# Spreading routing weights per token with two float32r products instead of one float32 product

## The chip, the cores and the metric

The kernel runs on one core of one Trainium2 chip. The metric is the device time of one execution in microseconds (us). An execution uses TensorE (PE, with its weight loads shown as PEld), VectorE (DVE), ScalarE (ACT), GpSimd (POOL) and SyncE (SP), which issues the transfers.

## The reference

Two transformer blocks in sequence on x of 256 tokens by 1024 features: a first block of two attention layers, then a second block with one attention layer and a PEER layer, a mixture of 16384 experts that are one neuron each. The change lies in the PEER layer, of which this is what is computed, with PEER_HEADS 8, PEER_KEYS 128 and PEER_TOPK 16:

```python
def chunk(xc):
    qh = (xc @ w_query).reshape(PEER_CHUNK, PEER_HEADS, PEER_QDIM)
    s1 = jnp.einsum('thd,hnd->thn', qh[..., :PEER_HALF], sub_keys[:, 0]).astype(jnp.float32)
    s2 = jnp.einsum('thd,hnd->thn', qh[..., PEER_HALF:], sub_keys[:, 1]).astype(jnp.float32)
    v1, i1 = lax.top_k(s1, PEER_TOPK)
    v2, i2 = lax.top_k(s2, PEER_TOPK)
    cand = (v1[..., :, None] + v2[..., None, :]).reshape(PEER_CHUNK, PEER_HEADS, PEER_TOPK * PEER_TOPK)
    vs, ci = lax.top_k(cand, PEER_TOPK)
    e1 = jnp.take_along_axis(i1, ci // PEER_TOPK, axis=-1)
    e2 = jnp.take_along_axis(i2, ci % PEER_TOPK, axis=-1)
    idx = e1 * PEER_KEYS + e2
    g = jax.nn.softmax(vs, axis=-1)
    u_sel = u_experts[idx]
    v_sel = v_experts[idx]
    z = jnp.einsum('td,thkd->thk', xc, u_sel)
    a = (jax.nn.gelu(z.astype(jnp.float32)) * g).astype(xc.dtype)
    return jnp.einsum('thk,thkd->td', a, v_sel)
```

Every token thus has 128 chosen experts (8 heads of 16), each with two indices e1 and e2 below 128 and a weight g.

## The kernel before

The kernel gathers no expert rows. It computes the PEER layer densely, for all 16384 experts, and multiplies by a matrix of weights that is zero where an expert was not chosen. One **u block** (`u_tile`, from line 1314) takes one value of e1: it loads the 128 rows of u with that e1 (512 KB), splits them into a high and a low float32r part (ACT makes `hi`, line 186, DVE makes `lo`, line 211, in two halves of 128x512), runs 24 products of 256 columns on PE (lines 239 to 241) and applies gelu on ACT (line 1322). The result, 128 values of e2 by 256 tokens, stays in `GA` for e1 below KA = 72. For the other 56 values it goes into a ring of tiles `ge`, and a transfer writes it to memory (`spill`, line 1366, transfer on line 1369).

Once the routing is done, the weights are **spread** (lines 1483 to 1504). For four tokens at a time, 64 groups in all, DVE compares a row of numbers 0 to 127 (`iof`) with the token's indices: `o2` (line 1489) holds ones where e2 fits and `o1` (line 1490, bfloat16) where e1 fits, with the 128 chosen slots on the partitions. ACT multiplies `o1` by the weights, one activation of 128x128 per token, into `og` (line 1492). PE multiplies `o2` by `og`, one float32 product of 128 columns per token (line 1493), which the chip runs as two instructions: the profile shows 512 of them for 256 tokens. The four tokens' results lie in one PSUM tile `ps`. DVE multiplies its first 72 values of e1 into `GA` (line 1496), and ACT copies the other 56 to `GB` (line 1497).

While this stage runs, PE also computes the u blocks that are left: after each group or two the loop on line 1498 asks for one more `spill`. The stretch in which groups and u blocks alternate is called **the stage** below. After it come the products with v, one value of e1 after the other.

A scheduler sets the order on each engine from the priorities in program order and the dependences between tiles, and each engine then runs its own list in order. A ring of tiles has a number of buffers (`bufs`); the writer of a buffer waits until its last reader is done. `o1`, `o2` and `og` have two buffers of four tokens each, `hi` and `lo` four each.

Of the kernel before, what the change touches and what calls it, by code (L numbers as in the profile page):

```python
# [9 lines left out]
F32 = mybir.dt.float32  # L10
F32R = mybir.dt.float32r
# [3 lines left out]
AF = mybir.ActivationFunctionType  # L15
OP = mybir.AluOpType
# [133 lines left out]
class Net:  # L150
# [1184 lines left out]
    def peer(self, r4, h):  # L1335
        nc, v, a = self.nc, self.nc.vector, self.a
# [13 lines left out]
        eT = [tp.tile([128, 256], F32, name=f"eT{i}") for i in range(2)]  # L1350
        gT = tp.tile([128, 256], F32, name="gT")
# [5 lines left out]
        def uu(n):  # L1357
            while n and self.nu < KA + KS:
                if self.nu < KA:
                    self.u_tile(self.nu, h, GA[:, self.nu, :])  # L1360
                else:
                    spill()
                self.nu += 1
                n -= 1

        def spill():
            ge = self.wp.tile([128, 256], F32, name="ge", tag="ge", bufs=3)
            self.u_tile(self.nu, h, ge)
            nc.sync.dma_start(zd[self.nu - KA], ge)
        with ExitStack() as er:  # L1370
            self.wp = self.pool("wr", stack=er)
            wp = self.wp
# [108 lines left out]
        self.wp = self.pool("wa", stack=eg)  # L1481
        wp = self.wp
        iob = iof[:, None, :].to_broadcast([128, 4, 128])
        for t0 in range(0, S, 4):
            ps = self.ps()
            o2 = wp.tile([128, 4, 128], F32, name="o2", tag="o2", bufs=2)
            o1 = wp.tile([128, 4, 128], BF, name="o1", tag="o1", bufs=2)
            og = wp.tile([128, 4, 128], F32, name="og", tag="og", bufs=2)
            v.tensor_tensor(o2, iob, eT[1][:, t0:t0 + 4, None].to_broadcast([128, 4, 128]), op=OP.is_equal)
            v.tensor_tensor(o1, iob, eT[0][:, t0:t0 + 4, None].to_broadcast([128, 4, 128]), op=OP.is_equal)  # L1490
            for j in range(4):
                nc.scalar.activation(og[:, j], o1[:, j], AF.Copy, scale=gT[:, t0 + j:t0 + j + 1])  # L1492
                nc.tensor.matmul(ps[:, j * 128:j * 128 + 128], o2[:, j], og[:, j], start=(j == 0), stop=(j == 3),  # L1493
                                 skip_group_check=True)
            pv = ps.rearrange("p (t e) -> p e t", t=4)
            v.tensor_tensor(GA[:, :, t0:t0 + 4], pv[:, 0:KA], GA[:, :, t0:t0 + 4], op=OP.mult)
            nc.scalar.copy(GB[:, :, t0:t0 + 4], pv[:, KA:])
            n = N_E1 - 2
            if self.nu < n and (self.nu - KA - KS) * S <= t0 * (n - KA - KS):
                spill()  # L1500
                self.nu += 1
        while self.nu < N_E1:
            spill()
            self.nu += 1
# [10 lines left out]
        for e1 in range(N_E1):  # L1515
            for e in range(max(KA, e1 + 1), min(N_E1, e1 + NGE)):
                if e not in spilled:

                    ge = spilled[e] = wp.tile([128, 256], F32, name="ge", tag="ge", bufs=NGE)
                    nc.sync.dma_start(ge, zd[e - KA])  # L1520
            if e1 == 8:
# [11 lines left out]
                for c in range(2):  # L1533
                    ps = self.ps()
# [4 lines left out]
            else:  # L1539
                A = spilled.pop(e1)  # L1540
                i = v.tensor_tensor(A, A, GB[:, e1 - KA, :], op=OP.mult)
# [131 lines left out]
```

## Time and profile before

| | |
|---|---|
| median of 3 runs | 1414.01 us (1412.24 to 1414.22) |
| the profiled execution's own time | 1413.74 us |
| its span, first to last instruction | 1412.0 us |
| PE busy over the span | 1366.8 us, 97% |
| DVE busy | 1023.2 us, 72% |
| ACT busy | 821.9 us, 58% |
| POOL busy | 21.9 us, 2% |
| mean granted clock of PE | 0.992 |
| transfers `zd<-ge`, issue to landing, median | 1.7 us |

A row of a timeline has the start in us from the start of the span, the duration in us (of all of them, where several are merged), the engine, the line, the operation, the tiles as output<-inputs without their numbers, the shape, and xN for N merged instructions; in brackets stands how long the engine had been idle and what ended that. A row on a source line has minimum, median and maximum duration in ns. The work on PE is pipelined: durations of neighbouring products overlap, so the price of a product in a stream is the distance between starts.

### The profile page before, as it was taken

What the parts mean: (1) busy time and instruction counts of PE and PEld (TensorE: products, weight loads), DVE (VectorE), ACT (ScalarE), POOL (GpSimd) and SP (SyncE); (2) the same over time, 40 slices, a digit from 0 to 9 for tenths busy, and PEclk for the clock granted to TensorE, in tenths of its full rate; (3) what the DMA queues carried; (4) which work ended last, traced back from release to release, by engine and by line L of the source; (5) the groups of instructions that cost most, each with busy time, mean ns of one, the idle gap of its engine ahead of it and who ended that gap; (6) DMA issues with size and microseconds to landing.
All of it is one profiled execution on the core that took longest, in us unless ns stands there. A gap on an engine that the chain in (4) does not pass through costs nothing.

```text
span 1412.0 us, 24444 instructions
## 1 busy us (share of the span) xinstructions
PE 1366.8 (97%) x8522; PEld 1120.8 (79%) x8522; DVE 1023.2 (72%) x2636; ACT 821.9 (58%) x1887; POOL 21.9 (2%) x27
## 2 busy tenths in 40 slices
PE   6999999999989998999999999999999999999997
PEld 2566666477767755999999999999998888888885
DVE  3585756388665656799999968888866666677777
ACT  2353656357646654555555568888865555555554
POOL 0000000000001100000000000000000000000001
PEclk9999999999999999999999999999999999999999
DMA  8577564553486766455555555554456665677773
GB/s 309 199 272 273 197 203 138 199 186 101 138 313 199 216 225 223 135 182 179 179 179 179 181 188 193 165 164 162 165 194 227 194 194 194 194 227 239 245 242 114
DMA packets 94875, 279.15 MB, mean 198 GB/s; under 512 B 11112, under 2 KB 30320, under 8 KB 94624
## 3 DMA queue, kind: packets, MB, share of 16 engines
q1 hardware_dynamic: 94752, 277.59, 59.6%
q8 instruction: 67, 1.10, 0.3%
q14 instruction: 56, 0.46, 0.1%
HBM read 267.80 MB, written 13.94 MB: 200 GB/s over the span
## 4 chain that ended last, share of the span: by engine, by line
PE 90%; DVE 4%; DMA 4%; ACT 1%; issue 1%; SPq 0%; ACTq 0%; DVEq 0%
PE ps L240 18%; PE ps L239 18%; PE ps L241 18%; PE acc L240 5%; PE acc L239 5%; PE acc L241 5%; PE psa L393 5%; PE ps L1493 4%; PE ps L706 2%; DMA raw<-in_w1o 1%; PE ps L725 1%; PE ps L701 1%; PE psa L365 1%; DMA adaw<-in_adaw 1%; DVE lo L211 1%; PE ps L631 1%
## 5 line engine op out<-in xcount | busy, mean ns | idle before, releaser
L186 ACT CAST hi<-raw 128x512 fp32r<-128x512 f32 (+1 forms) x700 | 429.4, 618 | 349.9 <-PE ps L240 147.1
L211 DVE TENSOR_TENSOR lo<-raw,hi 128x512 fp32r<-128x512 f32 (+1 forms) x700 | 479.8, 688 | 179.7 <-ACT hi L186 162.8
L239 PE MATMUL ps<-hh,hi 128*128 128x256 f32 x1160 | 333.0, 287 | 1.3 <-DVE hh L187 1.3
L240 PE MATMUL ps<-hl,hi 128*128 128x256 f32 x1160 | 328.3, 283 | 1.1 <-DVE hl L211 1.1
L241 PE MATMUL ps<-hh,lo 128*128 128x256 f32 x1160 | 328.4, 283 | 0.0
L239 PEld LDWEIGHTS ps<-hh,hi 128*128 128x128 f32 x1160 | 222.6, 192 | 1.5 <-issue 1.5
L240 PEld LDWEIGHTS ps<-hl,hi 128*128 128x128 f32 x1160 | 222.4, 192 | 1.3 <-DVE hl L211 1.3
L241 PEld LDWEIGHTS ps<-hh,lo 128*128 128x128 f32 x1160 | 222.2, 192 | 0.0
L239 PE MATMUL ps<-hi,Ah 128*128 128x512 f32 x508 | 198.1, 390 | 0.0
L240 PE MATMUL ps<-lo,Ah 128*128 128x512 f32 x508 | 197.7, 389 | 0.0
L241 PE MATMUL ps<-hi,Al 128*128 128x512 f32 x508 | 197.6, 389 | 0.0
L239 PEld LDWEIGHTS ps<-hi,Ah 128*128 128x128 f32 x508 | 95.4, 188 | 20.1 <-issue 0.2
L241 PEld LDWEIGHTS ps<-hi,Al 128*128 128x128 f32 x508 | 95.4, 188 | 19.9
L240 PEld LDWEIGHTS ps<-lo,Ah 128*128 128x128 f32 x508 | 95.4, 188 | 19.9 <-DVE lo L211 0.2
L1492 ACT ACTIVATE og<-o,gT 128x128 f32<-128x128 bf16 x256 | 87.2, 394 | 4.1 <-DVE o L1490 0.3
L393 PE MATMUL psa<-adaw,cond 128*32 128x512 f32 x320 | 81.3, 610 | 3.1 <-DMA adaw<-in_adaw 3.1
L240 PE MATMUL acc<-lo,hh 128*128 128x512 f32 (+1 forms) x176 | 70.7, 402 | 2.4 <-DVE lo L211 2.4
L239 PE MATMUL acc<-hi,hh 128*128 128x512 f32 (+1 forms) x176 | 69.6, 401 | 2.6 <-DVE hh L187 1.4
L241 PE MATMUL acc<-hi,hl 128*128 128x512 f32 (+1 forms) x176 | 69.9, 398 | 0.0
L1493 PE MATMUL ps<-og,o 128*128 128x128 f32 x512 | 65.2, 275 | 0.1
L1493 PEld LDWEIGHTS ps<-og,o 128*128 128x128 f32 x512 | 61.4, 192 | 0.3 <-ACT og L1492 0.3
L733 ACT ACTIVATE P<-P,nm 128x128 f32<-128x128 f32 (+1 forms) x96 | 42.6, 446 | 13.5 <-DVE nm L730 13.4
(397 smaller groups left out, 1929.8 us busy)
## 6 DMA issues: line engine op xcount, KB each, us to landing
raw<-in_u SPq DMA_DIRECT2D x128, 512.0 KB, 3.6
raw<-in_v SPq DMA_DIRECT2D x128, 512.0 KB, 4.3
adaw<-in_adaw SPq DMA_DIRECT2D x86, 512.0 KB, 4.9
raw<-in_w SPq DMA_DIRECT2D x48, 512.0 KB, 4.3
raw<-in_wq SPq DMA_DIRECT2D x16, 512.0 KB, 3.4
zd<-ge SPq DMA_DIRECT2D x56, 128.0 KB, 1.7
ge<-zd SPq DMA_DIRECT2D x56, 128.0 KB, 3.6
raw<-in_adaw SPq DMA_DIRECT2D x10, 512.0 KB, 7.0
```

The lines of the kernel that those rows point to most:

```text
L186: return self.nc.scalar.copy(out, in_)
L211: return self.nc.vector.tensor_tensor(lo, src, hi.bitcast(F32), op=OP.subtract)
L239: mm(out, a[0][asl], b[0][bsl], start=first, stop=False, **kw)
L240: mm(out, a[0][asl], b[1][bsl], start=False, stop=False, **kw)
L241: mm(out, a[1][asl], b[0][bsl], start=False, stop=last, **kw)
L365: nc.tensor.matmul(ps[32 * q:32 * q + 32], self.cond[:, k, :], raw[:, j * 512:(j + 1) * 512], start=(k == 0), stop=(k == NK - 1), tile_pos ...
L393: nc.tensor.matmul(ps[32 * q:32 * q + 32], self.cond[:, ci + k, :], raw[:, j * 512:(j + 1) * 512], start=(k == 0), stop=(k == NK - 1), til ...
L631: nc.tensor.transpose(pr[:P, i * 128:i * 128 + 128], s.rearrange("p a d -> p (a d)") if P == 128 else s, self.identr)
L706: nc.tensor.matmul(o[64 * a:64 * a + 64], v[br][kb][:, 2 * pair + a, :], pts[a], start=first, stop=False, tile_position=(0, 64 * a), skip_ ...
L733: nc.scalar.activation(Pb, Pb, AF.Exp, scale=-1.0, bias=nm[:, r, br:br + 1], accum_out=sums[:, r, br:br + 1])
L1492: nc.scalar.activation(og[:, j], o1[:, j], AF.Copy, scale=gT[:, t0 + j:t0 + j + 1])
L1493: nc.tensor.matmul(ps[:, j * 128:j * 128 + 128], o2[:, j], og[:, j], start=(j == 0), stop=(j == 3), skip_group_check=True)
```

## The change

The float32 product of a token becomes two float32r products onto the same sums: `o2` times the high part of the weighted `o1`, then `o2` times the low part. `o2` is written as float32r.

- The weights `gT` are split once into `gh` and a low part, which replaces `gT` in place.
- ACT makes the high part, as before one activation per token, now from `gh` into a tile `ogh` of one token with a ring of four buffers.
- POOL makes the low part `ogl`, four tokens in one instruction of 128x512, in a ring of two buffers.
- `o1` is written ahead of `o2`.
- The ring of `ge` has two buffers instead of three.

```diff
-            ge = self.wp.tile([128, 256], F32, name="ge", tag="ge", bufs=3)
+            ge = self.wp.tile([128, 256], F32, name="ge", tag="ge", bufs=2)
...
+        gh = wp.tile([128, 256], F32R, name="gh")
+        self.split_to(gh, gT.bitcast(F32R), gT)
+        gh, gl = gh.bitcast(F32), gT
         for t0 in range(0, S, 4):
             ps = self.ps()
-            o2 = wp.tile([128, 4, 128], F32, name="o2", tag="o2", bufs=2)
+            o2 = wp.tile([128, 4, 128], F32R, name="o2", tag="o2", bufs=2)
             o1 = wp.tile([128, 4, 128], BF, name="o1", tag="o1", bufs=2)
-            og = wp.tile([128, 4, 128], F32, name="og", tag="og", bufs=2)
+            og = wp.tile([128, 4, 128], F32R, name="ogl", tag="ogl", bufs=2)
+            v.tensor_tensor(o1, iob, eT[0][:, t0:t0 + 4, None].to_broadcast([128, 4, 128]), op=OP.is_equal)
             v.tensor_tensor(o2, iob, eT[1][:, t0:t0 + 4, None].to_broadcast([128, 4, 128]), op=OP.is_equal)
-            v.tensor_tensor(o1, iob, eT[0][:, t0:t0 + 4, None].to_broadcast([128, 4, 128]), op=OP.is_equal)
+            nc.gpsimd.tensor_tensor(og, o1, gl[:, t0:t0 + 4, None].to_broadcast([128, 4, 128]), op=OP.mult)
             for j in range(4):
-                nc.scalar.activation(og[:, j], o1[:, j], AF.Copy, scale=gT[:, t0 + j:t0 + j + 1])
-                nc.tensor.matmul(ps[:, j * 128:j * 128 + 128], o2[:, j], og[:, j], start=(j == 0), stop=(j == 3),
-                                 skip_group_check=True)
+                oh = wp.tile([128, 128], F32R, name="ogh", tag="ogh", bufs=4)
+                nc.scalar.activation(oh, o1[:, j], AF.Copy, scale=gh[:, t0 + j:t0 + j + 1])
+                for i, g in enumerate((oh, og[:, j])):
+                    nc.tensor.matmul(ps[:, j * 128:j * 128 + 128], o2[:, j], g, start=(j == 0 and i == 0),
+                                     stop=(j == 3 and i == 1), skip_group_check=True)
```

On PE, the list has a place where two groups follow one another without a u block between them; there are 14 such pairs. These are the rows of one pair before (`ps_9943` and `ps_9959` are the two groups, `ps_9906` and `ps_9976` the u blocks around them):

```order
L241 MATMUL ps_9906<-hh_5763,lo_9926 128x256
L1493 MATMUL ps_9943<-og_9946,o2_9944 128x128 [waits DVE_49,Activation_49]
L1493 MATMUL ps_9943<-og_9946,o2_9944 128x128 [waits Activation_49] x3
L1493 MATMUL ps_9959<-og_9962,o2_9960 128x128 [waits DVE_49,Activation_49]
L1493 MATMUL ps_9959<-og_9962,o2_9960 128x128 [waits Activation_49] x3
L239 MATMUL ps_9976<-hh_5763,hi_9979 128x256 [waits PE_49]
```

The same place now, the first group `ps_9991` and the head of the second, `ps_10016`:

```order
L1499 MATMUL ps_9991<-ogh_9998,o2_9992 128x128 [waits DVE_49,Activation_49]
L1499 MATMUL ps_9991<-ogl_9994,o2_9992 128x128 [waits Pool_49]
L1499 MATMUL ps_9991<-ogh_10002,o2_9992 128x128 [waits Activation_49]
L1499 MATMUL ps_9991<-ogl_9994,o2_9992 128x128
L1499 MATMUL ps_9991<-ogh_10006,o2_9992 128x128 [waits Activation_49]
L1499 MATMUL ps_9991<-ogl_9994,o2_9992 128x128
L1499 MATMUL ps_9991<-ogh_10010,o2_9992 128x128 [waits Activation_49]
L1499 MATMUL ps_9991<-ogl_9994,o2_9992 128x128
L1499 MATMUL ps_10016<-ogh_10023,o2_10017 128x128 [waits DVE_49,Activation_49]
L1499 MATMUL ps_10016<-ogl_10019,o2_10017 128x128 [waits Pool_49]
```

Groups and u blocks keep their places on PE: 50 places with a group or a pair, and 49 u blocks of 24 products between them. Each token has a high and a low product, and the first low product of a group waits for POOL.

On ACT, these are the rows before that make the weights of the pair (`og_9946` and `og_9962`); `ge_9851` is the gelu of the second u block ahead of the pair, and `ps_9889` is the group that stands between the two u blocks:

```order
L1492 ACTIVATE og_9946<-o1_9945,gT_5858 128x128 [waits DVE_49,PE_49]
L1492 ACTIVATE og_9946<-o1_9945,gT_5858 128x128 x2
L1497 COPY GB_9704<-ps_9835 128x56x4 [waits DVE_49]
L1492 ACTIVATE og_9946<-o1_9945,gT_5858 128x128
L186 CAST hi_9979<-raw_9977 128x512 [waits DMAHW4_49,PE_49]
L186 CAST hi_9995<-raw_9977 128x512 [waits PE_49]
L1322 ACTIVATE ge_9851<-ps_9852 128x256 [waits PE_49]
L1492 ACTIVATE og_9962<-o1_9961,gT_5858 128x128 [waits PE_49]
L1492 ACTIVATE og_9962<-o1_9961,gT_5858 128x128 x2
L1497 COPY GB_9704<-ps_9889 128x56x4 [waits DVE_49]
L1492 ACTIVATE og_9962<-o1_9961,gT_5858 128x128
```

And now (`ogh_9998` to `ogh_10010` are the first group of the pair, `ogh_10023` to `ogh_10035` the second; `ge_9953` is the gelu of the u block directly ahead of the pair):

```order
L1497 ACTIVATE ogh_9998<-o1_9993,gh_9711 128x128 [waits PE_49]
L1497 ACTIVATE ogh_10002<-o1_9993,gh_9711 128x128 [waits PE_49]
L1497 ACTIVATE ogh_10006<-o1_9993,gh_9711 128x128 [waits PE_49]
L1497 ACTIVATE ogh_10010<-o1_9993,gh_9711 128x128 [waits PE_49]
L1503 COPY GB_9704<-ps_9928 128x56x4 [waits DVE_49]
L186 CAST hi_10108<-raw_10106 128x512 [waits DMAHW7_49,PE_49]
L186 CAST hi_10124<-raw_10106 128x512 [waits PE_49]
L1322 ACTIVATE ge_9953<-ps_9954 128x256 [waits DMAHW4_49,PE_49]
L1497 ACTIVATE ogh_10023<-o1_10018,gh_9711 128x128 [waits PE_49]
L1497 ACTIVATE ogh_10027<-o1_10018,gh_9711 128x128 [waits PE_49]
L1497 ACTIVATE ogh_10031<-o1_10018,gh_9711 128x128 [waits PE_49]
L1497 ACTIVATE ogh_10035<-o1_10018,gh_9711 128x128 [waits PE_49]
```

The weights of a pair's second group stood behind the gelu of the second u block ahead of the pair. Now they stand behind the gelu of the u block directly ahead of it, and each activation has a wait for PE.

On DVE, this is the stretch of the same pair now (before, line 1490 for the groups to come stood behind the second line-1496 multiplication, not between the two, and did not wait for POOL):

```order
L1502 TENSOR_TENSOR GA_5855<-ps_9991,GA_5855 128x72x4 [waits PE_49]
L1493 TENSOR_TENSOR o2_10080<-iof_5859,eT1_5857 128x512 [waits DVE_49]
L1492 TENSOR_TENSOR o1_10144<-iof_5859,eT0_5856 128x512 [waits Activation_49,Pool_49]
L1502 TENSOR_TENSOR GA_5855<-ps_10016,GA_5855 128x72x4 [waits PE_49]
L1493 TENSOR_TENSOR o2_10143<-iof_5859,eT1_5857 128x512 [waits DVE_49]
L1492 TENSOR_TENSOR o1_10207<-iof_5859,eT0_5856 128x512 [waits Activation_49,Pool_49]
L211 TENSOR_TENSOR lo_10172<-raw_10169,hi_10171 128x512 [waits DMAHW2_49,PE_49,Activation_49]
```

The number of DVE instructions in the stage is the same but for the one split of `gT`. On POOL, which had nothing in the stage, there are now 64 multiplications of 128x512 in a row. SP's list of transfers is the same.

## Rows read from the trace of the kernel before

**Rows 1.** Busy time by stretch, sum of four stretches from 845 to 1045.

```profile
sum 200.00, PE 199.92 PEld 199.75 DVE 164.99 ACT 163.91 POOL 0.00; mean PE 49.98 PEld 49.94 DVE 41.25 ACT 40.98 POOL 0.00
```

**Rows 2.** Chain of waits from 815 to 1050: start, us, what, xN merged.

```profile
861.39 1.78 PE ps L1493 x16
...
926.12 0.89 PE ps L1493 x8
929.89 0.89 PE ps L1493 x8
...
1034.08 1.78 PE ps L1493 x16
```

**Rows 3.** Timeline of PE and PEld in early stages: float32r products of few columns.

```profile
328.30 0.56 PE L725 MATMUL ps<-kT,qT 128*128 128x128 f32 x4
137.11 1.87 PEld L878 LDWEIGHTS ps<-kT,qT 128*128 128x128 f32 x16
98.18 0.87 PE L631 MATMUL ps<-identr,qhl 128*128 128x128 f32 x8
```

**Rows 4.** Timeline of PE and ACT around the pair that starts at 933.49.

```profile
933.49 1.95 PE L1493 MATMUL ps<-og,o 128*128 128x128 f32 x16
933.63 0.62 ACT L186 CAST hi<-raw 128x512 fp32r<-128x512 f32 x1 [0.78 <-PE ps L240]
934.15 0.38 ACT L1322 ACTIVATE ge<-ps 128x256 f32<-128x256 f32 x1
934.58 0.99 ACT L1492 ACTIVATE og<-o,gT 128x128 f32<-128x128 bf16 x3
```

**Rows 5.** Timeline of ACT, a gelu with weights right behind it.

```profile
855.89 0.38 ACT L1322 ACTIVATE ge<-ps 128x256 f32<-128x256 f32 x1
856.17 0.98 ACT L1492 ACTIVATE og<-o,gT 128x128 f32<-128x128 bf16 x3
```

**Rows 6.** The first pair: chain of waits, then timelines of PE and ACT.

```profile
847.43 3.40 DMA zd<-ge
848.73 1.95 PE L1493 MATMUL ps<-og,o 128*128 128x128 f32 x16
850.92 0.35 ACT L1497 COPY GB<-ps 128x224 f32<-128x224 f32 x1 [2.94 <-DMA zd<-ge]
```

**Rows 7.** Timeline of DVE in the pair of rows 4.

```profile
934.89 0.45 DVE L1496 TENSOR_TENSOR GA<-ps,GA 128x288 f32<-128x288 f32 x1
935.26 0.68 DVE L1489 TENSOR_TENSOR o<-iof,eT 128x512 f32<-128x512 f32 x1
935.86 0.45 DVE L1496 TENSOR_TENSOR GA<-ps,GA 128x288 f32<-128x288 f32 x1
```

**Rows 8.** POOL's multiplications and additions: lines 1568 and 1107 by source line.

```profile
L1568 POOL TENSOR_TENSOR raw<-xr,gf x2: 1300/1302/1305, 1397.6 to 1399.5; 128x512 f32<-128x512 f32 x2
L1107 POOL TENSOR_TENSOR bb<-bb,cst x16: 636/642/1096, 453.4 to 492.9; 128x256 f32<-128x256 f32 x16
```

**Rows 9.** POOL and DVE at once, 487 to 494: timelines, and line 211 there.

```profile
487.47 1.09 POOL L1107 TENSOR_TENSOR bb<-bb,cst 128x256 f32<-128x256 f32 x1
488.52 1.09 POOL L1107 TENSOR_TENSOR bb<-bb,cst 128x256 f32<-128x256 f32 x1
L211 DVE TENSOR_TENSOR lo<-raw,hi x4: 890/1014/1124, 487.2 to 490.3; 128x512 fp32r<-128x512 f32 x4
490.61 2.89 POOL L1107 TENSOR_TENSOR bb<-bb,cst 128x256 f32<-128x256 f32 x4
491.65 0.70 DVE L1306 TENSOR_TENSOR ps<-ps,ona 128x512 f32<-128x512 f32 x1 [0.45 <-ACT osq L1305]
```

**Rows 10.** POOL and DVE at once near the end, timelines, and line 274 everywhere.

```profile
1401.67 1.27 POOL L1568 TENSOR_TENSOR gf<-xr,gf 128x512 f32<-128x512 f32 x1 [0.84 <-DVE rx L272]
1401.81 1.15 DVE L274 SCALAR_TENSOR_TENSOR rx<-rx 128x1 f32<-128x1 f32 x1
L274 DVE SCALAR_TENSOR_TENSOR rx<-rx x10: 211/219/1150, 13.7 to 1405.9; 128x1 f32<-128x1 f32 x10
```

## The prediction

> **What bounds the kernel now.** I read the busy time by stretch first, to see which engine has no slack while the routing weights are spread. From 845 to 1045 PE is busy 199.92 of 200 us, DVE 164.99, ACT 163.91 and POOL not at all [rows 1]. The chain of waits says the same and gives the beat: a group of four tokens takes 0.89 us on PE, single groups start 3.77 us apart, so a u block takes 2.88, and a pair takes 1.78 [rows 2]. Of these long pieces there are 13 from 861.39 to 1034.08, and the timeline has one more at 848.73 [rows 6]. The stage is thus 64 groups of 0.89 and 49 u blocks of 2.88, 57.0 + 141.1 = 198.1 us. A microsecond lost or won by PE here is one of the kernel's time; DVE has some 35 us to spare, ACT as much. Anything that makes PE wait, or that adds more than 35 us to DVE's list, shows in the end.
>
> **PE's own work.** A float32 product is two instructions, and a group's eight take 0.89 us, 0.111 each [rows 2]. The change also issues eight per group, float32r of 128 columns. The trace has just this form: four in a row last 0.56, the last of them 0.22 as its single ones do, so (0.56 - 0.22)/3 = 0.113 from start to start. With 16 columns it is no less: sixteen weight loads in 1.87, the last 0.19, so 1.68/15 = 0.112 [rows 3]. Columns do not set it; the load of the weights does, and it is repeated where two products in a row share them, as line 878's do (one `qT` for two `kT`); the low product will load `o2` again. I take +0.001 for each of 512, **+0.6 us**, with 0 and +1 as ends.
>
> **ACT's list and the ring `ogh`.** The 256 activations keep their shape, so they cost what they cost; the split of `gT` adds one instruction on ACT and one on DVE ahead of the stage, where both wait for PE: nothing. But `ogh` holds four tokens, not eight. The weights of the next group can only be made when PE has used those of the last, and in the new list the second group of a pair stands behind the gelu of the u block directly ahead. Singles have time: 2.88 us of u block. For a pair, count from PE's start T = 933.49 [rows 4]. ACT's cast starts at T + 0.14 and the gelu at T + 0.66; weights follow a gelu by 0.28 where nothing else holds them [rows 5], so at T + 0.94. The first lasts 0.40, the next follow every 0.295 ((0.99 - 0.40)/2). PE could start the second group at T + 0.89 and now starts at about T + 1.37, and then goes by 0.295 a token instead of 0.22, three times 0.07. That is 0.48 + 0.22 = 0.70 us a pair. In the first pair ACT stands at the copy of `GB`, which is done only once the transfer has landed, until 850.92 [rows 6]; behind it now come two casts and a gelu (0.25 + 0.52 + 0.52 + 0.28) before the second group's weights at 852.5, ready at 852.9, where PE wanted them at 848.73 + 0.89 = 849.62: 3.3 us. The ring alone thus costs 13 x 0.70 + 3.3 = **12.4 us**; if a pair's weights started as soon as PE lets go of the buffers, it would be some 0.25 a pair, 6.5 in all, the low end.
>
> **POOL beside DVE.** This decides. POOL's 64 instructions take 1.30 us each alone (128x512), 83 us where it has nothing else to do [rows 8], and each low part is asked for a u block or more before PE needs it. Its own time is hidden. What it does to DVE is not. While POOL's additions and the `lo` subtractions ran together, the two took turns: POOL's starts are 1.05 apart, its instructions grew from 0.642 to 1.09 and DVE's from 0.69 to 1.01 [rows 8, 9]. A DVE instruction of one column even lasted 1.15 instead of 0.219 because POOL held it [rows 10]. An instruction with one input in PSUM went past POOL untouched, 0.70 [rows 9]. So `o1`, `o2` and `lo`, all with two inputs in SBUF, take turns with POOL, and the multiplication into `GA` does not. One turn of POOL with 256 columns and one `lo` take 1.05, and `lo` alone takes 0.60 (the step of such instructions in [rows 7]), so POOL adds 0.45; 256 columns more add 1.302 - 0.642 = 0.66 [rows 8]. I take **1.10 us** of DVE's time per POOL instruction.
>
> The Trainium skill, on the page "SBUF — State Buffer" (Who interferes with whom), says that the pair of ports which VectorE's second input and GpSimd share is an exclusive lock for the whole instruction. By that each POOL instruction would cost DVE its whole 1.30 us, and the sum below would end 64 x 0.20 = 12.8 us later, at 1452; the turns above show that some 0.2 overlaps, and I go by them.
>
> DVE's list in the stage: 64 x (0.37 + 0.60 + 0.60) for `GA`, `o2`, `o1` [rows 7] and 98 `lo` of 0.60 are 159.3 us. POOL adds 64 x 1.10 = 70.4, together 229.7. Some `GA` run in POOL's shadow, because the same end of a group releases both: the second of each pair and those before DVE falls behind, some 20 x 0.37 = 7.4. That leaves 222.3. In the first pair DVE stands some 3.1 us with ACT, which can't be used: 225.4. DVE starts the stage ahead by what a single group leaves, about 1.5 us (its weights are ready at T + 2.2 of 3.77): 223.9. Against 198.1 that is **+25.8 us**.
>
> This replaces the ring's 12.4 rather than adding to it. Single groups alone would just fit: four instructions of 0.60 and one POOL turn with `GA` in its shadow are 3.50 to 3.60 of 3.77. But a pair asks DVE for 6 x 0.60 + 2 x 1.10 + 0.37 = 6.2 in 4.66 + 0.70 = 5.36 us. DVE is then late, its `GA` no longer falls into POOL's shadow, singles take 2.4 + 1.1 + 0.37 = 3.87, and the delay grows instead of shrinking. It reaches PE through ACT: the copy of `GB` waits for `GA`, and behind that copy stand casts, gelu and weights. So PE's waits at the pairs should grow from 0.7 to some 2 us.
>
> **The rest.** `o1` ahead of `o2`: both are made two groups or more ahead, nothing. `ge` with two buffers: a write lands after 1.7 us, and the next use of its buffer comes two u blocks later, over 5.7 us: nothing, unless SP is late by 4 us. SP's list is unchanged.
>
> Sum: 1413.74 (the profiled execution, 0.3 under the median shown) + 25.8 = **1439.5 us**.
>
> **The rivals.**
> 1. *Only the ring costs.* If POOL's turns fit into the 35 us that DVE has spare and into `GA`'s shadow (all 64: 23.7 us, so 229.7 - 23.7 = 206.0), the pairs bound: 12.4 + 0.6, 1426.7. For it: singles just fit. Against: the pairs do not.
> 2. *POOL is heavier* than its rows: its input is bfloat16 and its weight a broadcast, which no row shows. At 1.30 per turn and no `GA` hidden it is +20, 1460; at twice the length POOL itself becomes the beat and it is far more.
> 3. *Faster: float32r loads weights quicker.* Eight transposes in float32r, also 128 columns, take 0.87, the last 0.25: 0.089 each [rows 3]. At that rate the 512 products take 45.6 us instead of 57.0; were the ring and POOL hidden, 1413.7 - 11.4 = 1402.3. It decides if an ordinary product behaves like these; the row of line 725 says it does not. The Trainium skill has a rule of this kind on the page "TensorE: Matmul & The Clock Gate" (Back-to-back issue gap): pairs of load and product of 128 columns sustain about 81 ns. By it the products would take 41.5 us and the kernel 1398, an estimate; the trace's 113 ns speaks against it.
> 4. *No change*: PE's work is the same, and POOL and the ring are hidden by buffers that I judge too small: 1414.
>
> **How the numbers follow.** About 0.2% is what a measurement here can tell from no change. Forecast 0.56, ring only 0.22, POOL heavier 0.11, no change 0.05, faster 0.06. So faster 0.06, same 0.05, slower 0.89. The range runs from the ring's low end, 1413.7 + 6.5 = 1420, to just under rival 2's first price, 1458; it leaves out the faster case, no change and most of the heavy POOL, some 0.18.
>
> **What would show it.** Right: 512 float32r products at 0.112 apart; POOL busy over 83 us and each instruction well over 1.30; `o1`, `o2`, `lo` longer than 0.69; PE idle at the pairs, released by ACT's weights, growing over the first pairs; DVE nearly without idle time. Wrong: DVE's durations unchanged (then rival 1), PE waiting for POOL in single groups (rival 2), or products closer than 0.1 (rival 3).

## The result: slower by 0.9%, and the profile after

The changed kernel took 1428.29 us, median of 5 runs (1422.86 to 1430.27); the kernel before took 1414.01, now also of 5 (1412.24 to 1415.94). The ratio is 1.0094, 95% interval 1.0071 to 1.0117. That is slower, inside the range of 1420 to 1458, and 11.2 us under the forecast of 1439.5. Rival 1, in which only the ring costs, had 1426.7. The profiled execution took 1428.72 us, its span 1427.0.

The page of the changed kernel begins with busy time, share of the span and instructions of each engine:

```profile
PE 1375.7 (96%) x8522; PEld 1129.3 (79%) x8522; DVE 1053.7 (74%) x2637; ACT 821.3 (58%) x1888; POOL 100.5 (7%) x91
```

DVE gained 30.5 us against the table ahead, and POOL 78.6. The busy time by stretch, summed over 845 to 1045, answers to [rows 1]:

```profile
sum 200.00, PE 193.89 PEld 192.04 DVE 183.41 ACT 153.68 POOL 72.43; mean PE 48.47 PEld 48.01 DVE 45.85 ACT 38.42 POOL 18.11
```

PE, which had no idle time here, now waits 6.1 us, and DVE is not full. The list of waits from 845 to 1065 (total us, times, longest) names what PE waits for:

```profile
POOL ogl L1494 <- PE ps L1499: 112.7, 40, 17.8
...
PE ps L1499 <- ACT ogh L1497: 6.4, 14, 2.3
ACT GB L1503 <- DVE GA L1502: 4.9, 14, 0.8
```

Fourteen waits, one for each pair, all for ACT's weights, none for DVE or POOL. In a pair the timeline of PE and ACT reads:

```profile
913.74 0.22 PE L1499 MATMUL ps<-ogh,o 128*128 128x128 f32 x1
...
914.35 0.38 ACT L1322 ACTIVATE ge<-ps 128x256 f32<-128x256 f32 x1
914.47 0.28 PE L1499 MATMUL ps<-ogl,o 128*128 128x128 f32 x1
914.62 1.56 ACT L1497 ACTIVATE ogh<-o,gh 128x128 fp32r<-128x128 bf16 x5
...
915.07 0.33 PE L1499 MATMUL ps<-ogh,o 128*128 128x128 f32 x1 [0.32 <-ACT ogh L1497]
...
919.14 0.22 PE L1499 MATMUL ps<-ogh,o 128*128 128x128 f32 x1
```

From PE's start T = 913.74 the weights follow the gelu at T + 0.88, and PE starts the second group at T + 1.33. The forecast had T + 0.94 and T + 1.37. The next group starts at T + 5.40, where a pair and a u block took 1.78 + 2.88 = 4.66 [rows 2]: 0.74 us a pair, where the forecast had 0.70. It is the same at each of the 13 later pairs and does not grow.

In the first pair the timelines of ACT and PE answer to [rows 6], and the stretches behind them show PE's granted clock (the column after POOL's):

```profile
852.31 0.34 ACT L1503 COPY GB<-ps 128x224 f32<-128x224 f32 x1 [2.88 <-DMA zd<-ge]
854.32 0.33 PE L1499 MATMUL ps<-ogh,o 128*128 128x128 f32 x1 [2.27 <-ACT ogh L1497]
```

```profile
854.00:856.00 2.00, 1.68 (x13) 1.69 (x14) 2.00 (x5) 2.00 (x8) 0.00 (x0) 1.00 0.54 125
856.00:858.00 2.00, 2.00 (x13) 2.00 (x12) 2.00 (x4) 1.30 (x4) 1.04 (x1) 0.56 0.80 286
858.00:860.00 2.00, 2.00 (x13) 2.00 (x13) 1.00 (x2) 0.18 (x2) 0.00 (x0) 0.59 0.05 17
860.00:862.00 2.00, 2.00 (x20) 2.00 (x19) 1.39 (x3) 2.00 (x7) 1.04 (x1) 1.00 0.14 49
```

PE waited 2.27 us for the weights, and about 4 us of the next u block then went at a clock of 0.56 to 0.59, near the lower of its two levels, 1.2 of 2.4 GHz: 13 products in each 2 us, where 0.12 us from one to the next would make 16 or 17. That costs some 1.4 us more. The stage lasts 211.7 us (847.3 to 1059.0) instead of 198.2 (845.0 to 1043.2), 13.5 more: 13 x 0.74, 2.3 and 1.4 are 13.3 of them. It also began 2.3 us later, behind code that the change does not touch.

What POOL does to DVE shows in the same pair, timelines of DVE and POOL:

```profile
914.48 0.69 DVE L211 TENSOR_TENSOR lo<-raw,hi 128x512 fp32r<-128x512 f32 x1 [0.42 <-ACT hi L186]
914.83 1.24 POOL L1494 TENSOR_TENSOR ogl<-o,gT 128x512 fp32r<-128x512 bf16 x1 [2.53 <-PE ps L1499]
915.09 0.45 DVE L1502 TENSOR_TENSOR GA<-ps,GA 128x288 f32<-128x288 f32 x1
915.45 1.16 DVE L1493 TENSOR_TENSOR o<-iof,eT 128x512 fp32r<-128x512 f32 x1
```

POOL starts when PE is done with a group, because only then is its buffer free. DVE's next instruction is `GA`, released by the same event, with one input in PSUM, and it keeps its 0.45 us. Only `o2` behind it is held, until POOL ends at 916.07. Over the stage (845 to 1060, instructions by line: busy us, mean ns) nothing else on DVE grew:

```profile
L1493 DVE TENSOR_TENSOR o<-iof,eT 128x512 fp32r<-128x512 f32 x62 | 75.4, 1217 | 0.0
L211 DVE TENSOR_TENSOR lo<-raw,hi 128x512 fp32r<-128x512 f32 x101 | 68.1, 685 | 20.4 <-ACT hi L186 20.4
```

`o2` went from 681 ns in the kernel before to 1217: 0.53 us per group, where the forecast had 1.10 per POOL instruction.

### The profile page after: what moved, and what is told of

Its sections match the earlier page's. It is cut to its first block, busy times and chain, and to the rows that moved or that the text cites. A ratio compares the mean times of both kernels' runs of the same rounds, so it can differ in the third digit from the quotient of the medians.

```text
span 1427.0 us, 24570 instructions
## 1 busy us (share of the span) xinstructions
PE 1375.7 (96%) x8522; PEld 1129.3 (79%) x8522; DVE 1053.7 (74%) x2637; ACT 821.3 (58%) x1888; POOL 100.5 (7%) x91
## 4 chain that ended last, share of the span: by engine, by line
PE 90%; DMA 4%; DVE 4%; ACT 2%; issue 1%; SPq 0%; ACTq 0%; DVEq 0%
PE ps L239 18%; PE ps L240 18%; PE ps L241 18%; PE acc L240 5%; PE acc L239 5%; PE acc L241 5%; PE psa L393 5%; PE ps L1499 4%; PE ps L706 2%; DMA raw<-in_w1o 1%; PE ps L725 1%; PE ps L701 1%; PE ps L517 1%; DVE lo L211 1%; PE ps L631 1%; PE psa L365 1%
## 5 line engine op out<-in xcount | busy, mean ns | idle before, releaser
L1494 POOL TENSOR_TENSOR ogl<-o,gT 128x512 fp32r<-128x512 bf16 x64 | 78.6, 1229 | 482.3 <-DVE gT L211 333.9
L1497 ACT ACTIVATE ogh<-o,gh 128x128 fp32r<-128x128 bf16 x256 | 81.5, 393 | 0.0
L1493 DVE TENSOR_TENSOR o<-iof,eT 128x512 fp32r<-128x512 f32 x64 | 77.7, 1213 | 0.0
L1499 PE MATMUL ps<-ogh,o 128*128 128x128 f32 x256 | 61.4, 275 | 6.4 <-ACT ogh L1497 6.4
```

Of the source, the lines that this page charges most:

```text
L1494: nc.gpsimd.tensor_tensor(og, o1, gl[:, t0:t0 + 4, None].to_broadcast([128, 4, 128]), op=OP.mult)
L1497: nc.scalar.activation(oh, o1[:, j], AF.Copy, scale=gh[:, t0 + j:t0 + j + 1])
L1499: nc.tensor.matmul(ps[:, j * 128:j * 128 + 128], o2[:, j], g, start=(j == 0 and i == 0), stop=(j == 3 and i == 1), skip_group_check=True)
```

## The experiments

The theory after the result, R: the ring of four is the whole loss. Its rival, D: DVE, held by POOL, is late, and that is what the products wait for. Each run stands beside runs of the kernel before on its own chip, and its ratio is to these.

**Ring alone and POOL alone, in the kernel before.** `e2_before_ring4`:

```diff
-            og = wp.tile([128, 4, 128], F32, name="og", tag="og", bufs=2)
...
+                og = wp.tile([128, 128], F32, name="og", tag="og", bufs=4)
```

> The kernel before with its weighted one-hots as a ring of four one-token tiles, as ogh has, instead of two tiles of four tokens. No GpSimd work and no float32r is added. Theory R: the pairs pay as in the changed kernel, 13 x 0.70 + about 2.3 to 3.7 us at the first pair: 1425 to 1428 us, with ScalarE's og behind PE at every pair. Theory D: nothing else runs beside VectorE, so 1413 to 1416 us.

`e5_before_pool`:

```diff
+            xx = wp.tile([128, 4, 128], F32R, name="xx", tag="xx", bufs=1)
+            nc.gpsimd.tensor_tensor(xx, o1, gT[:, t0:t0 + 4, None].to_broadcast([128, 4, 128]), op=OP.mult)
```

> The kernel before with one GpSimd multiplication per group added (the low part's instruction of the changed kernel, a bfloat16 one-hot times the weights into a float32r tile of 512 columns), whose result nothing reads. The weighted one-hots keep their two tiles of four tokens. Theory R: VectorE loses about 0.5 us at one instruction per group and makes it up in its slack before the next: 1413 to 1417 us. Theory D, as the prediction had it (1.10 us of VectorE's time for every GpSimd instruction, and stalls that grow): 1425 to 1440 us. In the middle (1418 to 1424) would mean that VectorE's cover is only just long enough.

The ring alone: 1421.73 us, ratio 1.0055 (1.0037 to 1.0073). R's sign, but less than it said. From group to group a pair takes 5.18 us here, 0.52 too long instead of 0.74. The chain of waits in one pair shows why:

```profile
862.82 0.46 PE ps L1493 x4
863.28 0.36 ACT ge L1322
863.64 0.30 ACT og L1492
863.98 0.49 PE ps L1493 x2
864.59 0.22 PE ps L1493 x2
864.81 0.12 PE ps L240
864.93 0.44 PE ps L1493 x4
...
868.00 0.89 PE ps L1493 x8
```

The second group again stands behind gelu and weights, but in this kernel PE's list has products of the next u block (line 240) between its tokens, and they fill a part of the waits. In its first pair PE waited 1.37 us and kept its clock. POOL alone: 1438.26 us, ratio 1.0174 (1.0157 to 1.0192), and what the forecast had for the whole change. Its DVE, one single group:

```profile
907.58 2.13 DVE L211 TENSOR_TENSOR lo<-raw,hi 128x512 fp32r<-128x512 f32 x2
909.63 0.44 DVE L1498 TENSOR_TENSOR GA<-ps,GA 128x288 f32<-128x288 f32 x1
910.00 0.68 DVE L1489 TENSOR_TENSOR o<-iof,eT 128x512 f32<-128x512 f32 x1
910.86 0.69 DVE L1490 TENSOR_TENSOR o<-iof,eT 128x512 bf16<-128x512 f32 x1 [0.18 <-ACT og L1494]
```

Here nothing makes POOL wait for PE. It starts behind `o1`, lies beside the two `lo`, and the two steps take 2.05 us (907.58 to 909.63) instead of 1.20: 0.85 for one POOL instruction. With a short wait for ACT the single group takes 3.89 us on DVE (907.58 to the next `lo` at 911.47), more than PE's 3.77. So D is right in this kernel and R in the other, and the two costs had to be taken apart in the changed one.

**The changed kernel without POOL, with the short ring and with a long one.** `e3_no_pool`, and `e4_no_pool_ring8` with `bufs=8` besides:

```diff
+        og = wp.tile([128, 4, 128], F32R, name="ogl")
+        nc.gpsimd.memset(og.bitcast(F32), 0.0)
...
-            og = wp.tile([128, 4, 128], F32R, name="ogl", tag="ogl", bufs=2)
...
-            nc.gpsimd.tensor_tensor(og, o1, gl[:, t0:t0 + 4, None].to_broadcast([128, 4, 128]), op=OP.mult)
...
-                oh = wp.tile([128, 128], F32R, name="ogh", tag="ogh", bufs=4)
+                oh = wp.tile([128, 128], F32R, name="ogh", tag="ogh", bufs=8)
```

> The changed kernel without GpSimd's multiplication: the low products stay, but all read one constant tile of zeros, so the low part of the weights is left out of the sums. The ring of four stays. Theory R: still 1425 to 1430 us, the waits at the 14 pairs as before (14 to 15 us), while VectorE's o2 falls from 1.2 back to 0.69 us. Theory D: with VectorE undisturbed the loss goes, 1414 to 1417 us.

> The run e3_no_pool (the changed kernel without GpSimd's multiplication, its low part left out) with ogh as a ring of eight tiles instead of four. Theory R (in the changed kernel the ring is what PE waits for): neither the short ring nor GpSimd is left, and what remains are 512 products at 0.113 us where there were 512 passes at 0.111: 1413 to 1417 us, with PE busy 50 of 50 us in the stage. If 1422 or more, the float32r products themselves, or the earlier shift of 2.4 us at the start of the stage, cost more than the trace lets one see.

Without POOL: 1426.92 us, ratio 1.0091 (1.0074 to 1.0108), the changed kernel's own ratio. `o2` is back at 679 ns, and the waits of PE are those of the changed kernel:

```profile
PE ps L1499 <- ACT ogh L1497: 6.3, 14, 2.1
```

With a ring of eight besides: 1412.99 us, ratio 0.9991 (0.9978 to 1.0004), and PE is full again from 845 to 1045:

```profile
sum 200.00, PE 200.00 PEld 200.00 DVE 164.01 ACT 162.15 POOL 0.00; mean PE 50.00 PEld 50.00 DVE 41.00 ACT 40.54 POOL 0.00
```

This settles the loss of the change: the ring is all of it, POOL none that can be measured, and the 512 float32r products cost what the float32 instructions did. (With the longer ring the scheduler also puts `o1` one group further ahead on DVE, which has time for it; the order of the kinds in DVE's list stays.)

**The changed kernel with a long ring.** If so, lengthening the ring should win the loss back. `e1_ring7`, and later `e14_no_pool_ring7`, the same without POOL as in `e3_no_pool`:

```diff
-            ge = self.wp.tile([128, 256], F32, name="ge", tag="ge", bufs=2)
+            ge = self.wp.tile([128, 256], F32, name="ge", tag="ge", bufs=1)
...
-                oh = wp.tile([128, 128], F32R, name="ogh", tag="ogh", bufs=4)
+                oh = wp.tile([128, 128], F32R, name="ogh", tag="ogh", bufs=7)
```

> The changed kernel with ogh as a ring of seven tiles instead of four, and ge as one tile instead of two to make the space. Everything else, GpSimd's multiplication too, is as in the changed kernel. Theory R (the short ring is the whole loss: at each pair of groups ScalarE may not write the second group's first tile before the first group's first products are done): with seven tiles the first three tokens of the second group are made ahead and the fourth is needed 0.6 us later than before, so the 0.70 us at each of 13 pairs and most of the 2.3 us of the first pair go: 1414 to 1417 us. Theory D (VectorE, slowed by GpSimd, makes one-hots late, and that is what the products wait for): the ring does not matter, 1426 to 1430 us. If the single ge tile costs something, ScalarE's wait in front of ge shows it, and the time is higher than R says by that much.

> The run e1_ring7 without GpSimd's multiplication: ring of seven, one ge tile, and VectorE's list in the order that the longer ring gave it (both lo of a u block ahead of the next o1, where the changed kernel has o1 first); the low part of the weights is left out, its products read zeros. If the order of VectorE's list or the single ge tile made the 18 us of e1_ring7, they stay: 1428 us or more. If GpSimd made them, by lying on lo, they go: 1411 to 1417 us.

It does not: 1432.19 us, ratio 1.0132 (1.0113 to 1.0150), a miss for R. Without POOL it is 1416.88, ratio 1.0017 (1.0002 to 1.0032). So of the 1.3% that the long ring loses, 1.15 points are POOL's, in a kernel where POOL cost nothing while the ring was short. Two things besides the ring differ in both runs: the single `ge` tile, and the order of DVE's list, `lo`, `lo`, `o1` in place of `o1`, `lo`, `lo`. Without POOL they make at most the rest, and only in the first pair: in `e14_no_pool_ring7` it takes 7.71 us from group to group (4.90 before), every later pair 4.66. Whether POOL would cost as much with the long ring and the old order, no run shows. The timelines of DVE and POOL in `e1_ring7` show what is different:

```profile
912.77 0.45 DVE L1502 TENSOR_TENSOR GA<-ps,GA 128x288 f32<-128x288 f32 x1
913.14 0.68 DVE L1493 TENSOR_TENSOR o<-iof,eT 128x512 fp32r<-128x512 f32 x1
913.83 1.04 POOL L1494 TENSOR_TENSOR ogl<-o,gT 128x512 fp32r<-128x512 bf16 x1 [2.72 <-DVE o L1493]
914.15 1.86 DVE L211 TENSOR_TENSOR lo<-raw,hi 128x512 fp32r<-128x512 f32 x2 [0.33 <-ACT hi L186]
```

DVE is so late that this `GA` belongs to a group that PE finished long ago, and POOL's start, at the end of the next group (912.74 + 1.09, as T + 1.09 in the changed kernel; `o2`, which the bracket names, happens to end there too), falls behind `o2` and onto `lo`. The `lo` are on the way to PE, and so is `GA`: the copy of `GB` waits for it 53.1 us in 62 waits, 4.9 in 14 in the changed kernel. The pair that starts at 912.74 on PE takes 5.76 us to the next group at 918.50, more than with the short ring.

**Where POOL lies, with the ring of four.** `e10_pool_early` is `e3_no_pool` with POOL's instruction put back, into a tile that nothing reads; `e9_pool_phase` is the reverse in `e5_before_pool`, POOL held back by PE because its tile now shares a ring of three with `og`:

```diff
+            xx = wp.tile([128, 4, 128], F32R, name="xx", tag="xx", bufs=1)
+            nc.gpsimd.tensor_tensor(xx, o1, gl[:, t0:t0 + 4, None].to_broadcast([128, 4, 128]), op=OP.mult)
```

```diff
-            og = wp.tile([128, 4, 128], F32, name="og", tag="og", bufs=2)
+            og = wp.tile([128, 4, 128], F32, name="og", tag="og", bufs=3)
...
-            xx = wp.tile([128, 4, 128], F32R, name="xx", tag="xx", bufs=1)
+            xx = wp.tile([128, 4, 128], F32, name="xx", tag="og", bufs=3)
```

> The run e3_no_pool with GpSimd's multiplication put back, but into one tile that nothing reads, so that it need not wait for the products that read the tile two groups ago and starts as soon as its one-hot is made. The order of VectorE's and ScalarE's instructions and the ring of four are those of the changed kernel; the low part is left out of the sums as in e3_no_pool. Theory P (where GpSimd's instruction lies beside VectorE decides: in the changed kernel it starts at the end of a group, lies beside GA, which is not slowed, and beside o2 alone; started early it lies beside lo, which the next u block waits for): lo goes from 0.69 to over 1 us, VectorE falls behind, and the time is 1432 to 1442 us. Theory R (GpSimd is harmless in the changed kernel, wherever it lies): 1425 to 1430 us.

> The run e5_before_pool with GpSimd's idle multiplication held back to the end of the group before, as in the changed kernel: its unread tile takes turns with the weighted one-hots in one ring of three tiles of four tokens, so that it waits for the products of the group before to be read. Theory P: GpSimd's instruction then lies beside GA and o2, and a good part of the 25 us of e5_before_pool goes: 1414 to 1425 us. If VectorE's sum alone decides (0.37 + 1.09 + 0.60 + 1.22 us per single group against 3.77, but 2 x 2.06 to 2.3 + 1.22 per pair against 4.66), 1430 us or more. The shared ring moves a few of ScalarE's and VectorE's instructions at the pairs, which may cost some us of its own.

1429.67 us, ratio 1.0104 (1.0082 to 1.0126): with the ring of four, POOL costs no time that can be told from none (the interval takes in the 1.0091 of `e3_no_pool`) even where it lies on `lo`, which grew to 1010 ns. Theory P, that its place alone decides, falls. The stretches of this run show that no more would fit (columns PE, PEld, DVE, ACT, POOL):

```profile
950.00:1000.00 50.00, 48.84 (x408) 48.42 (x407) 50.00 (x70) 38.31 (x111) 18.99 (x16) 1.00 0.47 155
1000.00:1050.00 50.00, 48.42 (x404) 47.98 (x402) 50.00 (x69) 38.44 (x111) 18.98 (x16) 1.00 0.47 156
```

DVE is full and PE just begins to lose by it. The second run is inconclusive: 1431.03 us, ratio 1.0106 (1.0081 to 1.0131), 0.7 points better than `e5_before_pool`, but POOL waited for PE only 35 times, `lo` still took 932 ns on average, and the shared ring gave DVE's list another order at the pairs.

**How much cover, idle time of DVE that can take up a delay, is left in the changed kernel.** `e13_pool_twice`:

```diff
             nc.gpsimd.tensor_tensor(og, o1, gl[:, t0:t0 + 4, None].to_broadcast([128, 4, 128]), op=OP.mult)
+            nc.gpsimd.tensor_tensor(og, o1, gl[:, t0:t0 + 4, None].to_broadcast([128, 4, 128]), op=OP.mult)
```

> The changed kernel with GpSimd's multiplication issued twice in a row, the same result written twice. The order of every engine's list is otherwise the changed kernel's. Theory cover (in the changed kernel GpSimd costs VectorE 0.5 us per group and VectorE has some 17 us left in the stage): a second instruction lies on lo and o1 and costs VectorE 0.5 to 0.85 us per group, 32 to 54 us against 17, so 1443 to 1466 us. If GpSimd's instructions are harmless in this kernel wherever they lie, 1426 to 1431 us.

1461.81 us, ratio 1.0330 (1.0305 to 1.0355): the cover is gone. DVE has no idle time from 900 to 1050, `o2` stays at 1214 ns, and the second instruction lies on `lo` and `o1` (by line, 845 to 1090). Not all of the 33 us above the changed kernel is DVE's time: PE's waits are now so long that its granted clock falls again and again, to a mean of 0.93 in the first stretch below, where the changed kernel has 1.00; that is some 3 of its 50 us, an estimate from the missing 0.07.

```profile
900.00:950.00 50.00, 44.39 (x342) 43.90 (x341) 50.00 (x59) 32.54 (x95) 34.47 (x26) 0.93 0.39 128
...
sum 150.00, PE 132.24 PEld 130.82 DVE 150.00 ACT 98.90 POOL 102.60; mean PE 44.08 PEld 43.61 DVE 50.00 ACT 32.97 POOL 34.20
```

```profile
L211 DVE TENSOR_TENSOR lo<-raw,hi 128x512 fp32r<-128x512 f32 x98 | 101.6, 1073 | 4.6 <-ACT hi L186 4.6
...
L1492 DVE TENSOR_TENSOR o<-iof,eT 128x512 bf16<-128x512 f32 x61 | 54.9, 900 | 0.0
```

**Faster products, without POOL.** The weights as two bfloat16 parts, all operands of the products bfloat16. In `e7_bf16` DVE makes them token by token, in `e11_bf16_act` and `e12_bf16_dve` four tokens at a time, with indices and weights stored twice so that each operand has step 1:

```diff
+                v.tensor_scalar(o2[:, j], iob, eT[1][:, t], None, op0=OP.is_equal)
+                v.tensor_scalar(og[:, j, 0], iob, eT[0][:, t], gh[:, t], op0=OP.is_equal, op1=OP.mult)
+                v.tensor_scalar(og[:, j, 1], iob, eT[0][:, t], gT[:, t], op0=OP.is_equal, op1=OP.mult)
```

```diff
+            v.tensor_tensor(half(o1), iob, cols(e1d, t0), op=OP.is_equal)
+            v.tensor_tensor(half(o2), iob, cols(e2d, t0), op=OP.is_equal)
+            v.tensor_tensor(half(ol), half(o1), cols(gld, t0), op=OP.mult)
...
+                nc.scalar.activation(oh[:, j], o1[:, j], AF.Copy, scale=gh[:, t0 + j:t0 + j + 1])
```

> Another way to make the same products: the weights as two bfloat16 parts, and VectorE makes per token the one-hot o2 and both weighted one-hots in one instruction each (compare with a column, multiply by a column), 12 instructions of 128 columns per group, all bfloat16; ScalarE's four scalings and GpSimd's multiplication are gone. VectorE now needs per single group 0.37 (GA) + 1.22 (two lo) + 12 x d. If d is 0.13 us or less (a fifth of the 0.68 us of 512 columns), it stays under PE's period, and with bfloat16 products of 0.11 us the time is 1413 to 1416 us, at half of that 64 x 0.45 = 29 us less: 1385 to 1390 us. If d is 0.25 us, VectorE needs 4.6 us per group against 3.77 and sets the pace: 1414 + 50 x 0.8 + 14 x 3 = about 1500 us.

> A version meant to beat both kernels: the weights as two bfloat16 parts, every operand of the products bfloat16, no work on GpSimd, the weighted one-hots in two tiles of four tokens. VectorE makes o1, o2 and the low part, each 512 columns with all operands bfloat16 and step 1 (the indices and weights are stored twice, side by side); ScalarE makes the high part as before. In e7_bf16 a bfloat16 product came every 0.06 us, so PE needs 0.46 us per group instead of 0.89, 27 us less in all. VectorE needs 64 x (0.37 + 3d) + 98 x 0.60 us: if d stays 0.60, as for float32 operands, that is 198 us, as long as the stage of the kernel before, and the pairs stall, 1415 to 1430 us; if d halves to 0.30, it is 140 us, and ScalarE (some 156 us of 171) is next: 1387 to 1400 us.

> As e11_bf16_act, but VectorE makes the high part too, one more instruction of 512 bfloat16 columns per group, and ScalarE's four scalings go. VectorE needs 64 x (0.37 + 4d) + 98 x 0.60 us: at d = 0.30 that is 159 us of the 171 that PE needs, with ScalarE far from its limit: 1385 to 1395 us. At d = 0.60 it is 236 us and the time 1450 us or more.

`e7_bf16` took 1462.73 us, ratio 1.0335 (1.0309 to 1.0360): behind a small instruction with one column as operand the next starts 0.16 us later, behind one with two 0.22, the twelve of a group are too much for DVE, and PE, which waits in most groups, shows a granted clock of 0.93. `e11_bf16_act` took 1388.67 us, ratio **0.9813 (0.9781 to 0.9845)**, and `e12_bf16_dve` 1389.55, 0.9820 (0.9795 to 0.9845): both beat both kernels. In `e11_bf16_act`, DVE by line and PE in one group:

```profile
L1509 DVE TENSOR_TENSOR ogl<-o,gld 128x512 bf16<-128x512 bf16 x62 | 26.0, 420 | 0.0
L1508 DVE TENSOR_TENSOR o<-iob,e2d 128x512 bf16<-128x512 bf16 x62 | 25.9, 418 | 0.0
```

```profile
913.20 0.23 PE L1513 MATMUL ps<-ogh,o 128*128 128x128 bf16 x1
...
913.60 0.22 PE L1513 MATMUL ps<-ogl,o 128*128 128x128 bf16 x1
913.63 0.36 PE L239 MATMUL ps<-hh,hi 128*128 128x256 f32 x1
```

Eight products 0.057 us apart ((913.60 - 913.20)/7), half of 0.111; the load of 128 bfloat16 weights lasts 98 ns on average here where a float32 or float32r one lasts 191, which fits the prediction's reading that the load sets the pace. On DVE there are instructions of 0.42 us in place of 0.68, so that three of them cost less than two did (3 x 0.34 against 2 x 0.60 from start to start). The Trainium skill has the rule for these on the page "VectorE: DVE Perf Modes" (What auto-detection actually checks): two results per cycle if every tensor is 16 bits wide with step 1. The trace agrees: steps of 0.34 us instead of 0.60.

## Why the prediction was right in sign and range, and where its point failed

**PE's own work, +0.6: right.** `e4_no_pool_ring8` has the same 512 products and the time of the kernel before (0.9991); in the changed kernel they start 0.112 apart (910.03 to 910.70, six steps). Rival 3 is out.

**The ring, 12.4: right, and it is the whole loss.** T + 1.37 was T + 1.33, and 0.70 a pair was 0.74. The first pair had 3.3 and took 2.3 of waiting, with 1.4 behind it from the clock, which the working did not have. The ratios of `e3_no_pool` and `e4_no_pool_ring8` differ by 1.00%, 14 us.

**POOL beside DVE, 1.10 us each: mis-sized, and with it the step that decided.** Three numbers were off. An instruction of POOL's with a bfloat16 input takes 1.04 us where it is not held, not the 1.30 of the float32 row [rows 8]. Where it lies on `lo`, it costs DVE 0.85. And `GA`, 0.37, ran in its shadow in nearly all groups, not in some 20, because `ogl`'s two buffers tie POOL's start to the end of a group as `GA`'s is tied: 0.85 - 0.37 = 0.48, which is what `o2` shows (1.16 - 0.68). DVE's list is then 159.3 + 64 x 0.53 = 193 us, not 224, in a stage of 211.8.

The page "SBUF — State Buffer" of the Trainium skill (Who interferes with whom) has the shared ports as an exclusive lock. The trace bears that out for the order in time: `o2` at 915.45 ends where one of 0.5 to 0.6 us started at POOL's end, 916.07, would. For the price it is 0.85 of 1.04, some 0.2 less than the whole instruction, the same overlap that the prediction took from its own rows.

**"DVE is late, its `GA` no longer falls into POOL's shadow, and the delay grows", replacing the ring's 12.4: this step failed for the change.** With 0.48 a single group leaves DVE some 0.5 us of slack (0.37 + 1.09 + 0.60 + 1.22 = 3.28 of 3.77), and a pair asks for about 5.6 us; stretched by the ring itself to 5.40, it leaves DVE 0.2 us behind, which the next single makes up. The range held all the same, because it also took in rival 1, which had 0.22 of the chances; the mechanism that had 0.56 did not happen, so that for it the hit was luck. A mechanism of this kind does exist: in `e1_ring7` `GA` leaves the shadow as described, and POOL makes 16 us (against `e14_no_pool_ring7`), lost at the pairs (5.76 us to the next group, where singles keep 3.77 or 3.84). That it needs POOL is shown. That the length of the ring starts it is not: by the sums above a pair of 4.66 leaves DVE 0.9 us late, which the next two singles would just make up, and `e1_ring7` also has the other order on DVE. Why `e5_before_pool` loses 0.7 points more than `e10_pool_early`, with POOL in the same place, stays in part open: its trace shows no short ring that gives DVE time, a longer `lo` (1204 ns on average, 1010 there) and a wait of DVE for ACT's last weights (0.18 us in 33 waits), and I did not take these apart.

**The rest** held: no wait on `ge` or for the order of `o1` and `o2` shows in the waits of PE.

## What to carry to other kernels

Two delays in one loop need not add: a short ring that makes the bounding engine wait can give a slower neighbour the time it lacks, as with POOL's work, which cost nothing beside the ring of four. Removing the visible wait need not pay while the neighbour is slow: the run with the ring of seven, which also had another order on DVE, took 1432 us instead of 1428, and without POOL 1417. When an instruction moves to an engine that shares ports with a busy one, ask which event releases it and which instruction of the neighbour stands at that moment; beside `GA` and `o2` it cost DVE 0.48 us, on `lo` 0.85. And a rewrite that keeps the price of the bound operation (0.111 us per load of weights, float32 or float32r) had nothing to win here; the one that halved it (bfloat16, 0.057) did win.

## What was not expected of the hardware

- A single wait of 2.27 us on PE, with the clock at 1.00 since 600 at the latest, was followed by about 4 us at a granted clock of 0.56 to 0.59. `e3_no_pool` waited 2.1 us there and also shows less than the full clock (0.91 over 840 to 860); `e2_before_ring4` waited 1.37 us and kept it. The length of a single wait does not decide it: `e14_no_pool_ring7` waited 1.07 us there (shortly before, two starts were 0.36 apart instead of 0.11), and had 0.57 to 0.58 from 852 to 856.
- POOL's 128x512 multiplication takes 1.04 us with one bfloat16 input and a broadcast weight, 1.30 with two float32 inputs [rows 8].
- The scheduler's order of DVE's list changed with the buffers of tiles that DVE does not touch: `o1`, `lo`, `lo` with four or eight of `ogh` and two of `ge`, `lo`, `lo`, `o1` with seven and one. Which of the two did it, no run shows.
